# Ten of sixteen output-projection steps put inside the attention, and the value product one head at a time

## Chip, cores, metric

The kernel runs on one core of one Trainium2 chip. The metric is the device time of one execution in microseconds.

## What is computed

One inference step of a small hybrid decoder (two layers, width 1024) for a prompt of 512 tokens and 64 sample tokens (8 sequences of 8, each with 256 cached positions in pages). The change touches the first layer's mixer: eight heads of forgetting attention beside a gated recurrence, both halves multiplied by one output weight. Cut to what matters:

```python
s = einsum("bqhd,bkhd->bhqk", q, k) * scale
s = s + c_q - c_k                                    # running sums of log forget gates
prob = softmax(where(mask, s, NEG))
attn = einsum("bhqk,bkhd->bqhd", prob, v)
y_rg = h * gelu(gate)
merged = concatenate([attn, y_rg], axis=-1)          # 512 + 512 columns
x = x + einsum("bte,ed->btd", merged, w_out)
```

Products are in float32 accuracy: an operand is split into a high part and the rest, and high times high, high times low and low times high are summed.

## The kernel before

The text below names lines of the kernel before; in the kernel after, the same code stands further down. Tokens lie along the free dimension: `xT` holds 8 chunks of 128 model columns for 576 tokens, halved into 2 x 288. A program writes the order of instructions per engine; a scheduler shifts them by when it takes them to be ready, and each engine then works in that order.

The mixer's last stretch has three parts in program order.

1. *First half of the output projection* (`out_proj` with `k0 = 4`): weight rows that belong to the recurrence (`yh`, `yl`, the high and low parts of `y_rg`). For each of 8 output chunks `m`, `mm3` issues 24 matmuls of 128x288 (L132), and `add_x` adds the two halves to `xT` (VectorE, L658). Weights arrive as 1 MB (`raw`) and are split for two chunks at a time: a cast on ScalarE (L119), the rest on VectorE (L120), into a buffer `whl` of a pool with two buffers. Ahead of it, ScalarE and VectorE make the values' high and low parts (L461 to L463), and GpSimd builds the bias of the sample scores (L848 to L851).
2. *Attention*: 16 units, each one column `c` of two heads and one block `i` of 128 queries, `i` in the order 2, 3, 0, 1. In round n the code issues the scores of unit n (L787 the main product, L788 the gate sums through `kB`, L789 the mask), the softmax (VectorE L793, ScalarE L794, VectorE L795 and L796), then `p_trans` of unit n-1 (transposes L807, split into `ph` and `pl` by L809 and L810), then `p_out` of unit n-2: the value product (L821: for each key block `vh`x`ph`, `vl`x`ph`, `vh`x`pl`, both heads of the column against both heads' probabilities, 256 columns; half of the output is not used) and its split into `ah`, `al` (L829, L830). `kB` takes both buffers of the `whl` pool, four heads each. Between these pieces a list `side` spreads the sample group's attention: page loads by GpSimd (L743), their transposes (L873), products (all through L856), query copies on GpSimd (L762) and the transposes of its output (`sov`, L937).
3. *Second half of the output projection* (`k0 = 0`) over `ah`, `al`, again L132; chunk by chunk it hands on to the next norm.

Of the kernel before, what the change touches and what calls it, by code (L numbers as in the profile page):

```python
# [8 lines left out]
F32 = mybir.dt.float32  # L9
F32R = mybir.dt.float32r  # L10
# [8 lines left out]
P = 128  # L19
D = 1024  # L20
NP = 512
# [22 lines left out]
class Trunk:  # L44
# [343 lines left out]
    def mixer_ab(self):  # L388
# [3 lines left out]
        with tc.tile_pool(name="mix", bufs=1, reuse_waits="tile") as mp, ExitStack() as att:  # L392
# [8 lines left out]
            with tc.tile_pool(name="yy", bufs=1, reuse_waits="tile") as yp:  # L401
                with tc.tile_pool(name="rg", bufs=1, reuse_waits="tile") as rp:
# [7 lines left out]
                    for a in range(2):  # L410
                        for j, t in enumerate((self.xgh[a], self.xgl[a])):
# [57 lines left out]
                def prepare(m):  # L469
                    if m == 3:  # L470
                        q2s[2] = self.p_split(mp, *self.UNITS[2])
                    if m == 5:
# [256 lines left out]
    def k_rows(self, kT, ck, a):  # L729


        kB = self.wh.tile([P, 4, NP], F32R, name="kB", tag="whl")

        def step(h):
            self.nc.vector.tensor_copy(kB[0:64, h], kT[0:64, 4 * a + h, :])
            self.nc.scalar.copy(kB[64:68, h], ck[32 * h:32 * h + 4, a, :])

        return kB, [lambda h=h: step(h) for h in range(4)]
# [25 lines left out]

    UNITS = [(c, i) for c in range(4) for i in (2, 3, 0, 1)]


    def attention(self, mp, aq, q2s, zs, kT, cq, ck, vh, vl, qn, kn, vs, lf, ds, ah, al):
        nc, I = self.nc, self.I
        V, A, G, PE = nc.vector, nc.scalar, nc.gpsimd, nc.tensor  # L770
        with self.tc.tile_pool(name="at", bufs=2, reuse_waits="tile") as ap:
# [3 lines left out]
            kBs, ksteps = zip(*[self.k_rows(kT, ck, a) for a in range(2)])  # L775
            for f in ksteps[0]:
                f()
            obank = {}

            def p_scores(c, i, z):  # L780
# [3 lines left out]
                for e in range(2):  # L784
# [3 lines left out]
                    PE.matmul(s[:, 0:n], z[0:68, 1, e], kBs[h // 4][0:68, h % 4, 0:n], start=False, stop=False)  # L788
# [11 lines left out]
            def p_trans(c, i, es):  # L800
                n = (i + 1) * P
                ph = ap.tile([P, 4, 2, P], F32R, name="ph", tag="ph")
                pl = ap.tile([P, 4, 2, P], F32R, name="pl", tag="pl")
                for e in range(2):
                    pe = self.bank()
                    for k in range(i + 1):
                        PE.transpose(pe[:, k * P:(k + 1) * P], es[e][:, k * P:(k + 1) * P], self.ident)  # L807
                    pv = pe[:, 0:n].rearrange("p (k q) -> p k q", q=P)
                    A.copy(ph[:, 0:i + 1, e, :], pv)  # L809
                    V.tensor_tensor(pl[:, 0:i + 1, e, :], pv, ph[:, 0:i + 1, e, :].bitcast(F32), SUB)  # L810
                return ph, pl

            def p_out(c, i, ph, pl):
                if i % 2 == 0:
                    obank[0] = self.bank()
                o = obank[0]
                u = slice(i % 2 * 256, i % 2 * 256 + 256)
                cs = slice(c * P, (c + 1) * P)
                for k in range(i + 1):
                    for j, (v, p) in enumerate(((vh, ph), (vl, ph), (vh, pl))):  # L820
                        PE.matmul(o[:, u], v[:, k, cs], p[:, k].rearrange("p e q -> p (e q)"),  # L821
                                  start=(k == 0 and j == 0), stop=(k == i and j == 2))
                if i % 2 == 1:
                    t0 = (i - 1) * P
                    for e in range(2):
                        r = slice(e * 64, (e + 1) * 64)
                        src = o[r].rearrange("p (i e q) -> p i e q", i=2, e=2)[:, :, e, :]
                        dh, dl = [t[r, c, t0:t0 + 256].rearrange("p (i q) -> p i q", i=2) for t in (ah, al)]
                        A.copy(dh, src)  # L829
                        V.tensor_tensor(dl, src, dh.bitcast(F32), SUB)  # L830
# [12 lines left out]
            bn = one(full, "bn")  # L843
# [126 lines left out]
            for h in range(4):  # L970
                at(3 + h, ksteps[1][h])
            q1 = q2 = None
            for n in range(len(units) + 2):
# [14 lines left out]
                q1, q2 = nxt, t2  # L988

# [529 lines left out]
```

## Time and profile before

| | |
|---|---|
| median of 3 runs | 1306.14 us (1304.78 to 1307.19) |
| the profiled execution: time | 1310.66 us |
| the profiled execution: span from first to last instruction | 1308.9 us |
| mean granted TensorE clock | 0.995 |
| first half of the output projection | about 181.0 to 208.6 us |
| attention | about 208.6 to 296.3 us |

The profile is of one execution. A window row gives a stretch, its length, how long TensorE, its weight load, VectorE (DVE), ScalarE (ACT) and GpSimd (POOL) were busy in it with the number of instructions, then the granted TensorE clock, the DMA share and GB/s; a timeline row gives start, length and, in brackets, how long the engine sat idle just before and what released it. Lengths of matmuls overlap, so their rate is read from starts or from a count over a stretch.

### The profile page before, as it was taken

How to read it: one execution, taken by the hardware profiler on the slowest of the kernel's cores; microseconds unless marked ns; L12 is line 12 of the kernel's file. 1: busy time of each engine (PE TensorE's matmuls, PEld its weight loads, DVE VectorE, ACT ScalarE, POOL GpSimd, SP SyncE). 2: the span in 40 equal slices, each digit the busy share in tenths (PEclk: the TensorE clock that was granted, in tenths of full speed). 3: DMA queues.
4: the chain of work that ended last, by engine and by line, in shares of the span. 5: the costliest groups of instructions: out<-in, count | busy, mean ns of one | idle time of the engine just before them, and what ended most of it. 6: DMA issues, size and time to landing. Idle time of an engine off the chain costs nothing.

```text
span 1308.9 us, 23023 instructions
## 1 busy us (share of the span) xinstructions
PE 1288.2 (98%) x9462; PEld 1233.3 (94%) x9462; DVE 813.9 (62%) x1559; ACT 532.8 (41%) x877; POOL 167.4 (13%) x527
## 2 busy tenths in 40 slices
PE   8999999999999999999999999999999999999998
PEld 6987888779999999999999999899999999999998
DVE  6847847887767635765367657776743666346742
ACT  6656445674433313332133335444321343124421
POOL 2240053446100000000000002210000000000000
PEclk9999999999999999999999999899999999999999
DMA  6223232424233132312321212232223222223121
GB/s 175 85 67 101 78 130 81 122 60 130 71 100 105 38 97 97 99 65 68 110 83 36 66 50 82 84 131 66 68 67 129 65 82 70 79 97 99 34 92 49
DMA packets 105918, 111.64 MB, mean 85 GB/s; under 512 B 6722, under 2 KB 96970, under 8 KB 105805
## 3 DMA queue, kind: packets, MB, share of 16 engines
q1 hardware_dynamic: 101668, 101.68, 24.2%
q0 software_dynamic: 3072, 8.46, 2.3%
q8 instruction: 74, 1.21, 0.4%
q14 instruction: 32, 0.25, 0.1%
q10 hardware_dynamic: 1072, 0.04, 0.1%
HBM read 104.14 MB, written 6.25 MB: 84 GB/s over the span
## 4 chain that ended last, share of the span: by engine, by line
PE 90%; DVE 5%; ACT 3%; issue 1%; DMA 0%; ACTq 0%
PE mmb L132 77%; PE mmb L564 4%; PE mmb L856 2%; DVE whl L120 1%; PE mmb L821 1%; PE mmb L346 1%; PE mmb L807 1%; DVE xl L282 0%; ACT zh L1098 0%; ACT whl L119 0%; DVE xl L463 0%; PE mmb L494 0%; PE mmb L570 0%; DVE xT L1128 0%; ACT eb L794 0%
## 5 line engine op out<-in xcount | busy, mean ns | idle before, releaser
L132 PE MATMUL mmb<-xh,whl 128*128 128x288 f32 x3456 | 616.5, 298 | 3.3 <-DVE whl L120 1.7
L132 PEld LDWEIGHTS mmb<-xh,whl 128*128 128x128 f32 x3456 | 513.9, 190 | 7.0 <-DVE whl L120 2.2
L132 PE MATMUL mmb<-xl,whl 128*128 128x288 f32 x1728 | 372.6, 297 | 1.6 <-DVE xl L282 1.6
L119 ACT CAST whl<-wraw 128x1024 fp32r<-128x1024 f32 (+1 forms) x176 | 183.1, 1041 | 374.0 <-PE mmb L132 271.6
L132 PEld LDWEIGHTS mmb<-xl,whl 128*128 128x128 f32 x1728 | 280.1, 190 | 2.1 <-DVE xl L282 2.1
L132 PE MATMUL mmb<-hh,whl 128*128 128x288 f32 x1536 | 271.2, 297 | 0.1
L120 DVE TENSOR_TENSOR whl<-wraw,whl 128x1024 fp32r<-128x1024 f32 (+1 forms) x176 | 214.7, 1220 | 79.6 <-ACT whl L119 74.2
L132 PEld LDWEIGHTS mmb<-hh,whl 128*128 128x128 f32 x1536 | 226.2, 188 | 0.7 <-ACT hh L1237 0.6
L132 PE MATMUL mmb<-hl,whl 128*128 128x288 f32 x768 | 165.0, 296 | 0.0
L658 DVE TENSOR_TENSOR xT<-mmb,xT 128x288 f32<-128x288 f32 x128 | 52.6, 452 | 158.9 <-PE mmb L132 158.6
L1217 DVE TENSOR_TENSOR u<-mmb,rb 128x288 f32<-128x288 f32 x96 | 44.0, 458 | 135.4 <-PE mmb L132 127.4
L1222 POOL COPY ut<-u 128x18 f32<-128x18 f32 x96 | 23.1, 241 | 782.3 <-DVE u L1219 782.3
L132 PEld LDWEIGHTS mmb<-hl,whl 128*128 128x128 f32 x768 | 123.1, 188 | 0.0
L1237 ACT CAST hh<-hf 128x576 fp32r<-128x576 f32 x48 | 32.3, 674 | 139.0 <-DVE hf L1234 139.0
L1226 ACT ACTIVATE t<-u,par 128x592 f32<-128x592 f32 x96 | 84.6, 881 | 3.6 <-POOL u L1221 2.0
L1228 DVE SCALAR_TENSOR_TENSOR t<-u,par,t 128x592 f32<-128x592 f32 x96 | 80.1, 835 | 3.4
L1227 DVE SCALAR_TENSOR_TENSOR t<-u,par,t 128x592 f32<-128x592 f32 x96 | 79.6, 830 | 1.1 <-ACT t L1226 1.0
L1231 ACT ACTIVATE t<-t 128x592 f32<-128x592 f32 x48 | 33.6, 699 | 95.0 <-DVE t L1228 95.0
L1238 DVE TENSOR_TENSOR hl<-hf,hh 128x576 fp32r<-128x576 f32 x48 | 36.4, 759 | 34.8 <-ACT hh L1237 34.8
L564 PE MATMUL mmb<-whl,xh 128*128 128x512 f32 x192 | 53.7, 400 | 0.0
L564 PEld LDWEIGHTS mmb<-whl,xh 128*128 128x128 f32 x192 | 35.9, 191 | 8.2
L1218 DVE TENSOR_TENSOR u<-mmb,rb 128x224 f32<-128x224 f32 x96 | 36.6, 382 | 0.0
(383 smaller groups left out, 1311.4 us busy)
## 6 DMA issues: line engine op xcount, KB each, us to landing
wraw<-in_ffn_w_up SPq DMA_DIRECT2D x48, 1024.0 KB
wraw<-in_ffn_w_down SPq DMA_DIRECT2D x24, 1024.0 KB
wraw<-in_ab_w_in SPq DMA_DIRECT2D x9, 1024.0 KB
wraw<-in_ab_w_out SPq DMA_DIRECT2D x4, 1024.0 KB
xt<-in_x_prompt SPq DMA_DIRECT2D x4, 512.0 KB
out_y_p<-y SPq DMA_DIRECT2D x8, 256.0 KB
wraw<-in_ab_w_in SPq DMA_DIRECT2D x2, 512.0 KB
out_k_p<-X SPq DMA_DIRECT2D x1, 1024.0 KB
```

The lines of the kernel that those rows point to most:

```text
L119: keep(self.nc.scalar.copy(hi, v))
L120: keep(self.nc.vector.tensor_tensor(lo, v, hi.bitcast(F32), SUB))
L132: nc.tensor.matmul(ps[hf][:, 0:HT], w[:, k, :], x[:, hf * HT:(hf + 1) * HT], start=(n == 0 and j == 0), stop=(n == K - 1 and j == 2))
L564: PE.matmul(ps[i], x[:, i * P:(i + 1) * P], w[:, k2, :], start=(k == 0 and j == 0), stop=(k == 7 and j == 2))
L658: self.nc.vector.tensor_tensor(x, ps[hf][:, 0:HT], x, ADD)
L1217: V.tensor_tensor(u[:, 2:2 + HT], ps[0][:, 0:HT], self.rb[:, 0:HT], MUL)
L1218: V.tensor_tensor(u[:, 2 + HT:514], ps[1][:, 0:NP - HT], self.rb[:, HT:NP], MUL)
L1226: A.activation(t, u[:, 2:594], AF.Identity, scale=self.fw(l, 2, ch), bias=self.fb(l, ch))
L1227: V.scalar_tensor_tensor(t, u[:, 1:593], self.fw(l, 1, ch), t, MUL, ADD)
L1228: V.scalar_tensor_tensor(t, u[:, 0:592], self.fw(l, 0, ch), t, MUL, ADD)
L1231: A.activation(tg[:, 0:592], tg[:, 0:592], AF.Gelu_apprx_tanh)
L1238: V.tensor_tensor(hl, hf_, hh.bitcast(F32), SUB)
```

## The change

- The first half of the projection is made of 16 steps (`out_steps`): a chunk and a half of the tokens, 12 matmuls, one bank, one addition. Six run ahead of the attention. Ten are issued inside it, one each in rounds 4, 5, 6, 8, 10, 12, 14, 15, 16 and 17, right after the scores. The weight split is made per chunk (512 columns) into one buffer `fw`, double-buffered inside; `kB` has the other buffer of the pool, holds four heads, and is written over head by head.
- The value product goes one head at a time. A key block's weights are the high and low parts of one head side by side (`v2`, 2 x 64 columns), so `ph` and `pl` each pass once; two query blocks go together (256 columns, 128 for the last key block, whose first query block is masked). The two 64-row halves of the output are added afterwards: a copy on ScalarE and an addition on VectorE per head, then one split into `ah`, `al` for both. It runs before `p_trans` of the next unit, and for odd `i` only.
- The descriptor scratch of GpSimd's DMAs is set to 2048 bytes, and the sample bias `bn` moves to another pool.

```diff
@@ mixer_ab @@
-                vh, vl = [self.half(n, 1).rearrange("p c t -> p (c t)")[:, 0:2048].rearrange("p (i d) -> p i d", i=4)
-                          for n in ("xh", "xl")]
+                v2 = [t.rearrange("p c t -> p (c t)")[:, i * 1024:(i + 1) * 1024].rearrange("p (h s d) -> p h s d", h=H, s=2)
+                      for t in (self.half("xh", 1), self.half("xl", 1)) for i in range(2)]
...
-                    A.activation(vh[:, i, :], pv[i], AF.Identity, scale=sc)
+                    hd = lambda t: t.rearrange("p (h d) -> p h d", h=H)
+                    A.activation(v2[i][:, :, 0], hd(pv[i]), AF.Identity, scale=sc)
                     A.activation(vt[:, i, :], pv[i], AF.Identity, scale=sc)
-                    V.tensor_tensor(vl[:, i, :], vt[:, i, :], vh[:, i, :].bitcast(F32), SUB)
+                    V.tensor_tensor(v2[i][:, :, 1], hd(vt[:, i, :]), v2[i][:, :, 0].bitcast(F32), SUB)
...
-                self.out_proj(lambda k: (yh[:, k, :], yl[:, k, :]), 4, range(8), prepare)
-            self.attention(mp, aq, q2s, zs, kT, cq, ck, vh, vl, qn, kn, vs, lf, ds, ah, al)
-            att.close()
+                kB = self.wh.tile([P, 4, NP], F32R, name="kB", tag="whl")
+
+                fill = self.out_steps(lambda k: (yh[:, k, :], yl[:, k, :]), 4, range(8), prepare)
+                for _ in range(2 * self.AHEAD):
+                    fill.popleft()()
+                self.attention(mp, aq, q2s, zs, kT, cq, ck, v2, qn, kn, vs, lf, ds, ah, al, kB, fill)
+                att.close()
@@ new function @@
+    def out_steps(self, xs, k0, order, after):
+
+        w = self.I["ab_w_out"][0].rearrange("(k p) n -> p k n", p=P)
+        now = {}
+
+        fw = self.wh.tile([P, 2, 2, 512], F32R, name="fw", tag="whl")
+
+        def step(m, hf):
+            if hf == 0 and m % 4 == 0:
+                now["r"] = self.raw(w[:, k0:k0 + 4, m * P:m * P + 512], 4, 512)
+            hi, lo = [fw[:, m % 2, a].rearrange("p (k n) -> p k n", k=4) for a in range(2)]
+            if hf == 0:
+                v = now["r"][:, :, m % 4 * P:m % 4 * P + P]
+                self.nc.scalar.copy(hi, v)
+                self.nc.vector.tensor_tensor(lo, v, hi.bitcast(F32), SUB)
+            ps = self.bank()
+            for k in range(4):
+                xh, xl = xs(k)
+                for j, (a, x) in enumerate(((hi, xh), (hi, xl), (lo, xh))):
+                    self.nc.tensor.matmul(ps[:, 0:HT], a[:, k, :], x[:, hf * HT:(hf + 1) * HT],
+                                          start=(k == 0 and j == 0), stop=(k == 3 and j == 2))
+            x = self.xT[:, m, hf * HT:(hf + 1) * HT]
+            self.nc.vector.tensor_tensor(x, ps[:, 0:HT], x, ADD)
+            if hf:
+                after(m)
+
+        return deque([lambda m=m, hf=hf: step(m, hf) for m in order for hf in range(2)])
@@ k_rows, one head at a time @@
+    def k_rows(self, kB, kT, ck, h):
+
+        self.nc.vector.tensor_copy(kB[0:64, h % 4], kT[0:64, h, :])
+        self.nc.scalar.copy(kB[64:68, h % 4], ck[32 * (h % 4):32 * (h % 4) + 4, h // 4, :])
@@ attention @@
+    AHEAD = 3
+    FILL = (4, 5, 6, 8, 10, 12, 14, 15, 16, 17)
...
-                ph = ap.tile([P, 4, 2, P], F32R, name="ph", tag="ph")
-                pl = ap.tile([P, 4, 2, P], F32R, name="pl", tag="pl")
+                if i % 2 == 0:
+                    pair[c, i // 2] = [ap.tile([P, 4, 2, 2, P], F32R, name=nm, tag=nm, bufs=1) for nm in ("ph", "pl")]
+                ph, pl = pair[c, i // 2]
...
             def p_out(c, i, ph, pl):
+
                 if i % 2 == 0:
-                    obank[0] = self.bank()
-                o = obank[0]
-                u = slice(i % 2 * 256, i % 2 * 256 + 256)
-                cs = slice(c * P, (c + 1) * P)
-                for k in range(i + 1):
-                    for j, (v, p) in enumerate(((vh, ph), (vl, ph), (vh, pl))):
-                        PE.matmul(o[:, u], v[:, k, cs], p[:, k].rearrange("p e q -> p (e q)"),
-                                  start=(k == 0 and j == 0), stop=(k == i and j == 2))
...
+                    return
+                o = self.bank()
+                for e in range(2):
+                    for k in range(i + 1):
+                        w = v2[k][:, 2 * c + e].rearrange("p s d -> p (s d)")
+                        q0 = P if k == i else 0
+                        for j, p in enumerate((ph, pl)):
+                            PE.matmul(o[:, e * 256 + q0:e * 256 + 256], w,
+                                      p[:, k, e].rearrange("p i q -> p (i q)")[:, q0:256],
+                                      start=(k == 0 and j == 0), stop=(k == i and j == 1))
+                t = self.sm.tile([P, T], F32, name="fo", tag="dgs", bufs=1)[:, 0:256]
+                for e in range(2):
+                    r, x = [slice(a * 64, (a + 1) * 64) for a in (e, 1 - e)]
+                    u = slice(e * 256, e * 256 + 256)
+                    A.copy(t[r], o[x, u])
+                    V.tensor_tensor(t[r], o[r, u], t[r], ADD)
+                dh, dl = [x[:, c, (i - 1) * P:(i + 1) * P] for x in (ah, al)]
+                A.copy(dh, t)
+                V.tensor_tensor(dl, t, dh.bitcast(F32), SUB)
...
             for h in range(4):
-                at(3 + h, ksteps[1][h])
+                at(4 + 4 * (h // 2) + h % 2, lambda h=h: self.k_rows(kB, kT, ck, 4 + h))
...
                 step(k)
+                if n in self.FILL:
+                    fill.popleft()()
+                if q2:
+                    p_out(*q2)
                 t2 = (q1[0], q1[1], *p_trans(*q1)) if q1 else None
                 step(k)
-                if q2:
-                    p_out(*q2)
...
-    nc = bacc.Bacc("TRN2", target_bir_lowering=False, num_devices=1)
+    nc = bacc.Bacc("TRN2", target_bir_lowering=False, num_devices=1, dynamic_dma_scratch_size=2048)
```

How the order of instructions moves is shown at three places. In the kernel after, L683 is the addition of a step, L675 the `fw` split, L680 its matmuls, L855 the value product, L863 and L866 the addition and split of its output.

VectorE, ahead of the attention, before (`xl<-vt` is the values' low part, `xT` an addition, `whl` a weight split of two chunks):

```order
L722 COPY z<-cq 4x128 x4
L463 TENSOR_TENSOR xl<-vt,xh 128x512 x3
L658 TENSOR_TENSOR xT<-mmb,xT 128x288 x2
L463 TENSOR_TENSOR xl<-vt,xh 128x512
L725 CAST z<-mmb 64x256 x2
L120 TENSOR_TENSOR whl<-wraw,whl 128x1024
L658 TENSOR_TENSOR xT<-mmb,xT 128x288 x2
L710 TENSOR_TENSOR q_1991<-X,q_1991 128x2x64
L120 TENSOR_TENSOR whl<-wraw,whl 128x1024
```

and after:

```order
L756 COPY z<-cq 4x128 x4
L465 TENSOR_TENSOR xh<-vt,xh 128x8x64 x2
L465 TENSOR_TENSOR xl<-vt,xl 128x8x64
L683 TENSOR_TENSOR xT<-mmb,xT 128x288 x2
L465 TENSOR_TENSOR xl<-vt,xl 128x8x64
L759 CAST z<-mmb 64x256 x2
L744 TENSOR_TENSOR q_1905<-X,q_1905 128x2x64
L683 TENSOR_TENSOR xT<-mmb,xT 128x288 x2
L675 TENSOR_TENSOR fw<-wraw,fw 128x512
L744 TENSOR_TENSOR q_2032<-X,q_2032 128x2x64
L683 TENSOR_TENSOR xT<-mmb,xT 128x288
L675 TENSOR_TENSOR fw<-wraw,fw 128x512
```

The split that the third chunk needs (the first `fw` row here) still stands behind the values, the query copies and the additions of two chunks; it is half as wide.

VectorE, from the last unit's softmax to the end of the attention, before:

```order
L795 RECIPROCAL st<-st 128x1
L120 TENSOR_TENSOR whl<-wraw,whl 128x1024
L796 TENSOR_SCALAR eb<-eb,st 128x256
L795 RECIPROCAL st<-st 128x1
L810 TENSOR_TENSOR pl<-mmb,ph 128x128
L796 TENSOR_SCALAR eb<-eb,st 128x256
L830 TENSOR_TENSOR xl<-mmb,xh 64x256
L947 TENSOR_TENSOR xl<-mmb,xh 64x4x2x8
L810 TENSOR_TENSOR pl<-mmb,ph 128x2x128 x2
L830 TENSOR_TENSOR xl<-mmb,xh 64x256
```

and after:

```order
L822 TENSOR_REDUCE st<-mmb 128x1 x2
L120 TENSOR_TENSOR whl<-wraw,whl 128x1024
L824 RECIPROCAL st<-st 128x1 x2
L683 TENSOR_TENSOR xT<-mmb,xT 128x288
L825 TENSOR_SCALAR eb<-eb,st 128x256 x2
L863 TENSOR_TENSOR fo<-mmb,fo 64x256
...
L683 TENSOR_TENSOR xT<-mmb,xT 128x288
L120 TENSOR_TENSOR whl<-wraw,whl 128x1024
L863 TENSOR_TENSOR fo<-mmb,fo 64x256 x2
L866 TENSOR_TENSOR xl<-fo,xh 128x256
```

An addition of a step has come between the reciprocals and the scalings, and a second weight split stands ahead of the last three operations on `fo`.

TensorE, the tail of the attention, before (`sov` is the sample output, `eb` the probabilities of a prompt unit):

```order
L821 MATMUL mmb<-pl,xh 128x256
L807 MATMUL mmb<-ident,eb 128x128
L821 MATMUL mmb<-ph,xh 128x256
L821 MATMUL mmb<-ph,xl 128x256
L821 MATMUL mmb<-pl,xh 128x256
L937 MATMUL mmb<-ident,sov 128x128 x4
L807 MATMUL mmb<-ident,eb 128x128 x4
L821 MATMUL mmb<-ph,xh 128x256
L821 MATMUL mmb<-ph,xl 128x256
L821 MATMUL mmb<-pl,xh 128x256
```

and after:

```order
L855 MATMUL mmb<-pl,xl 128x128
L838 MATMUL mmb<-ident,eb 128x128 x2
L973 MATMUL mmb<-ident,sov 128x128 x4
L680 MATMUL mmb<-yh,fw 128x288
L680 MATMUL mmb<-yl,fw 128x288
...
L680 MATMUL mmb<-yh,fw 128x288
L838 MATMUL mmb<-ident,eb 128x128 x4
L680 MATMUL mmb<-yh,fw 128x288
L680 MATMUL mmb<-yl,fw 128x288
...
L855 MATMUL mmb<-pl,xh 128x128
L132 MATMUL mmb<-xh,whl 128x288 x2
```

Between the `sov` transposes and the last value product two steps of the projection (24 matmuls of L680) have come in; before, the wait for the probabilities lay there. The second half (L132) now begins only behind the last value product.

## Rows read from the trace of the kernel before

**Rows 1.** The page, busy us of the engines (share, instructions).

```profile
PE 1288.2 (98%) x9462; PEld 1233.3 (94%) x9462; DVE 813.9 (62%) x1559; ACT 532.8 (41%) x877; POOL 167.4 (13%) x527
```

**Rows 2.** Busy windows, projection's first half: stretch, length, us busy by engine.

```profile
181.00:188.00 7.00, 7.00 (x55) 6.87 (x52) 6.32 (x9) 5.37 (x11) 6.50 (x5) 1.00 0.43 154
188.00:190.00 2.00, 0.28 (x2) 0.18 (x2) 1.97 (x4) 1.77 (x3) 1.69 (x2) 1.00 0.49 121
190.00:208.60 18.60, 18.60 (x141) 18.60 (x142) 8.79 (x20) 5.08 (x9) 4.98 (x11) 1.00 0.47 163
```

**Rows 3.** Busy windows of the attention, cut at units 0, 4, 8, 12.

```profile
209.40:225.40 16.00, 15.71 (x138) 12.79 (x137) 14.18 (x46) 13.12 (x40) 5.69 (x12) 1.00 0.22 67
225.40:250.00 24.60, 24.06 (x233) 18.66 (x231) 22.30 (x69) 16.64 (x54) 11.12 (x18) 1.00 0.39 107
250.00:275.10 25.10, 24.27 (x261) 19.30 (x259) 20.24 (x62) 16.66 (x56) 7.01 (x8) 1.00 0.27 76
275.10:296.30 21.20, 18.77 (x181) 14.19 (x179) 18.73 (x57) 14.97 (x48) 13.12 (x55) 1.00 0.32 100
```

**Rows 4.** Timeline of TensorE at 190 us: start, us, instructions [wait, releaser].

```profile
189.82 0.81 PE L132 MATMUL mmb<-yh,whl 128*128 128x288 f32 x4 [1.72 <-DVE whl L120]
```

**Rows 5.** Timeline of VectorE, 180 to 190 us.

```profile
180.32 0.92 DVE L722 CAST z<-cq 4x128 fp32r<-4x128 f32 x4 [2.15 <-ACT vs L451]
...
186.89 0.84 DVE L463 TENSOR_TENSOR xl<-vt,xh 128x512 fp32r<-128x512 f32 x1
187.76 0.75 DVE L725 CAST z<-mmb 64x256 fp32r<-64x256 f32 x2
188.54 1.23 DVE L120 TENSOR_TENSOR whl<-wraw,whl 128x1024 fp32r<-128x1024 f32 x1
189.68 0.82 DVE L658 TENSOR_TENSOR xT<-mmb,xT 128x288 f32<-128x288 f32 x2
```

**Rows 6.** Timeline of ScalarE, query casts and kB copies.

```profile
188.21 0.70 ACT L726 CAST z<-mmb 64x256 fp32r<-64x256 f32 x2 [1.84 <-DVE z L725]
...
208.79 2.50 ACT L736 CAST kB<-ck 4x512 fp32r<-4x512 f32 x4 [3.87 <-PE mmb L132]
```

**Rows 7.** VectorE's groups by line and shape: count, busy us, mean ns.

```profile
L658 DVE TENSOR_TENSOR xT<-mmb,xT 128x288 f32<-128x288 f32 x128 | 52.6, 452 | 158.9 <-PE mmb L132 158.6
...
L830 DVE TENSOR_TENSOR xl<-mmb,xh 64x256 fp32r<-64x256 f32 x16 | 6.7, 418 | 1.2 <-ACT xh L829 1.0
...
L463 DVE TENSOR_TENSOR xl<-vt,xh 128x512 fp32r<-128x512 f32 x4 | 5.2, 1337 | 0.6 <-ACT vt L462 0.6
...
L120 DVE TENSOR_TENSOR whl<-wraw,whl 128x512 fp32r<-128x512 f32 x4 | 2.8, 690 | 0.0
```

**Rows 8.** The chain of waits in the attention: start, us, what.

```profile
272.63 1.41 PE mmb L821 x12
```

**Rows 9.** Timeline of TensorE, score matmuls of 128 columns.

```profile
263.51 0.27 PE L788 MATMUL mmb<-kB,z 68*128 68x128 f32 x1
263.63 0.23 PE L789 MATMUL mmb<-maskb,identb 128*128 128x128 bf16 x1
```

**Rows 10.** Timeline of TensorE in the tail of the attention.

```profile
288.67 0.23 PE L789 MATMUL mmb<-maskb,identb 128*128 128x128 bf16 x1
...
292.53 0.41 PE L807 MATMUL mmb<-ident,eb 128*128 128x128 f32 x2 [1.45 <-DVE st L795]
...
293.85 0.29 PE L132 MATMUL mmb<-xh,whl 128*128 128x288 f32 x1
...
295.87 0.29 PE L132 MATMUL mmb<-xh,whl 128*128 128x288 f32 x1
...
296.32 0.67 PE L132 MATMUL mmb<-xh,whl 128*128 128x288 f32 x3 [0.16 <-ACT xh L946]
```

**Rows 11.** Timeline of GpSimd, sample bias and query copies.

```profile
182.38 1.59 POOL L851 TENSOR_TENSOR bd<-cbs,ds 128x512 f32<-128x512 f32 x1
...
195.37 1.65 POOL L762 COPY qz<-qn 64x16 f32<-64x16 f32 x7 [4.56 <-DMA cache_v<-in_cache_v,pidx]
```

More of the change, by code (lines that the diff above doesn't have):

```diff
@@ L727, in p_prep @@
         return z
[L729 to L738, printed above, removed]
+    def k_rows(self, kB, kT, ck, h):
+        self.nc.vector.tensor_copy(kB[0:64, h % 4], kT[0:64, h, :])
+        self.nc.scalar.copy(kB[64:68, h % 4], ck[32 * (h % 4):32 * (h % 4) + 4, h // 4, :])
     def page(self, pool, src, j, bufs):
@@ L763, in s_queries, with attention @@
                                            qn[r, c, pr * 16:(pr + 1) * 16].rearrange("p (b t) -> p b t", b=2))
+    AHEAD = 3
+    FILL = (4, 5, 6, 8, 10, 12, 14, 15, 16, 17)
     UNITS = [(c, i) for c in range(4) for i in (2, 3, 0, 1)]
-    def attention(self, mp, aq, q2s, zs, kT, cq, ck, vh, vl, qn, kn, vs, lf, ds, ah, al):
+    def attention(self, mp, aq, q2s, zs, kT, cq, ck, v2, qn, kn, vs, lf, ds, ah, al, kB, fill):
         nc, I = self.nc, self.I
@@ L774, in attention @@
             units = self.UNITS
[L775 to L778, printed above, removed]
+            for h in range(4):
+                self.k_rows(kB, kT, ck, h)
+            pair = {}
             def p_scores(c, i, z):
@@ L787, in p_scores @@
                     PE.matmul(s[:, 0:n], z[:, 0, e], kT[:, h, 0:n], start=True, stop=False)
-                    PE.matmul(s[:, 0:n], z[0:68, 1, e], kBs[h // 4][0:68, h % 4, 0:n], start=False, stop=False)
+                    PE.matmul(s[:, 0:n], z[0:68, 1, e], kB[0:68, h % 4, 0:n], start=False, stop=False)
                     PE.matmul(s[:, qs], self.identb, self.maskb, start=False, stop=True)
@@ L808, in p_trans @@
                     pv = pe[:, 0:n].rearrange("p (k q) -> p k q", q=P)
-                    A.copy(ph[:, 0:i + 1, e, :], pv)
-                    V.tensor_tensor(pl[:, 0:i + 1, e, :], pv, ph[:, 0:i + 1, e, :].bitcast(F32), SUB)
+                    hi, lo = [t[:, 0:i + 1, e, i % 2, :] for t in (ph, pl)]
+                    A.copy(hi, pv)
+                    V.tensor_tensor(lo, pv, hi.bitcast(F32), SUB)
                 return ph, pl
@@ L814, in p_out @@
                 if i % 2 == 0:
-                    obank[0] = self.bank()
-                o = obank[0]
-                u = slice(i % 2 * 256, i % 2 * 256 + 256)
-                cs = slice(c * P, (c + 1) * P)
-                for k in range(i + 1):
-                    for j, (v, p) in enumerate(((vh, ph), (vl, ph), (vh, pl))):
-                        PE.matmul(o[:, u], v[:, k, cs], p[:, k].rearrange("p e q -> p (e q)"),
-                                  start=(k == 0 and j == 0), stop=(k == i and j == 2))
[L823 to L830, printed above, removed]
+                    return
[17 more added lines that the diff above has]
+                V.tensor_tensor(dl, t, dh.bitcast(F32), SUB)
             one = lambda shape, nm, dt=F32: aq.tile(shape, dt, name=nm, tag=nm, bufs=1)
@@ L842, in attention @@
             bd = one([P, 2, NB, H, NT], "bd")
-            bn = one(full, "bn")
+            bn = self.sm.tile([P, NB, H, NT], F32, name="bn", tag="sq", bufs=2)[0:NS]
             def s_setup():
@@ L983, in attention @@
                 step(k)
+                if n in self.FILL:
+                    fill.popleft()()
+                if q2:
+                    p_out(*q2)
                 t2 = (q1[0], q1[1], *p_trans(*q1)) if q1 else None
                 step(k)
-                if q2:
-                    p_out(*q2)
                 q1, q2 = nxt, t2
+            while fill:
+                fill.popleft()()
     def pool_setup(self, pb):
```

4 lines of the change are left out of this document (2 added, 2 removed).

## Prediction

> **What bounds the kernel now.** The first part of the page says that TensorE is busy for 98% of the span [rows 1], so a change can only gain where TensorE waits or where it is given less to do. Everything that is moved lies between 181.0 and 296.3 us, and I read that region by its windows first and by the timelines after. In the projection's first half TensorE is full but for two microseconds: between 188 and 190 us it works 0.28 us while VectorE works 1.97 [rows 2]. In the attention I cut the windows at the first score matmul of units 0, 4, 8 and 12. TensorE is idle for 0.29, 0.54, 0.83 and 2.43 us of the four stretches, 4.1 us together, and VectorE is busy for 89, 91, 81 and 88% of them [rows 3]. So the attention is a stretch in which two engines are nearly full at once. That is the point to keep: filling TensorE's holes costs VectorE work, and VectorE has little room.
>
> Then the timelines. From 190 us to the end of the first half, 141 matmuls take 18.60 us [rows 2], 0.132 each; a step (one chunk of 128 output columns, one half of the tokens, 12 matmuls) is 1.6 us. The stall at 188 us ends at 189.82 with VectorE's weight split L120 [rows 4], which starts at 188.54 because VectorE had the low parts of the values (L463) and the query copies (L725) ahead of it [rows 5].
>
> **Stretch 1, before the attention: -15.2 us.** Ten of sixteen steps leave it. The other six keep their pace, but the stall stays. Four steps end at 181.0 + 4 x 1.60 = 187.4. The fifth needs the third weight split, `fw`. On ScalarE its cast stands behind the query casts that end at 188.9 [rows 6]; on VectorE it stands behind L463, L725, a query split and the two additions of the second chunk, which as in [rows 5] end near 189.6. The split of 512 columns is 0.69 us [rows 7], so TensorE goes on at about 190.25, against 189.82 before. Two more steps end at 193.4. The old end is 208.6, 16 steps and the stall after 181.0 [rows 2]. The four copies of kB that now come earlier fall into the 2.15 us in which VectorE waited for `vs` [rows 5]; I cost them at nothing. Without that cover each would be about 0.4 us, as the half-width L830 is [rows 7].
>
> **Stretch 2, units 0 to 3: -0.9 us.** There is no fill here. The value product of units 0 and 1 gets shorter. Twelve old products take 1.41 us [rows 8], 0.118 each. Per column of heads the old code has 30 of 256 columns; the new one has 16 of 256 and 8 of 128. No row has just this product at 128 columns, so I bound it: half of 0.118 from below (0.059), 0.12 from above, the step from one 128-column matmul to the next in the scores [rows 9]. I take 0.12, since the row has the same width and type. A pair of units (2,3) then goes from 21 x 0.118 = 2.48 to 1.90, a pair (0,1) from 1.06 to 0.95: 0.58 and 0.11 less, 2.8 us over the attention (4.7 at the other bound). The first pair (2,3) falls into this stretch: -0.58. Before, four kB copies of ScalarE also stand ahead of the first exponential, from 208.79 for 2.50 us [rows 6]; they are no longer there. Since TensorE is idle for only 0.29 us of this stretch, I count half of that and 0.2 for the copies; the bound is the whole 1.9 us from 209.4 to 211.3.
>
> **Stretch 3, units 4 to 7: +3.85 us.** Three fills are 4.8 us of TensorE. Two value products give back 0.69, and I let half of the 0.54 us of waits be filled. VectorE gets three additions (0.45 us each [rows 7]), two `fw` splits and two extra half additions of L863 (0.42 each by L830 [rows 7]); one 1.23-us split of the second projection half, which stood here, moves to the end. That is 22.3 + 2.3 = 24.6 us in 28.4, 87% against 91% before, so VectorE doesn't become the bound.
>
> **Stretch 4, units 8 to 11: +2.1 us.** Two fills, 3.2, less 0.69 for the products and half of 0.83.
>
> **Stretch 5a, units 12 to 14 up to the last scores at 288.8: +2.8 us.** Two fills, 3.2, less 0.11 and half of the 0.55 us of waits that lie here.
>
> **Stretch 5b, the tail: +2.3 us.** Before, 288.8 to 296.3 is 7.5 us, in which nine matmuls (1.2 us) of the second half were already done [rows 10]. TensorE's order after is: fill 1.6, 16 products 1.9, two transposes 0.2, four `sov` transposes 0.4, fill 1.6, four transposes 0.45, fill 1.6, eight products 0.95. Together 8.7 us, and 8.7 + 1.2 - 7.5 = 2.3. Three fills (4.8) thus cost 2.3: here is the 1.45-us wait for L795 [rows 10], a reciprocal that stands behind a split L120 in VectorE's queue, and the first fill covers it. VectorE has some 7.1 us of work ahead of the last products: the split 1.2, two fill additions 0.9, three operations on `fo` 1.2, some 3.8 for softmax, probability splits and small copies (estimated from the 0.42 of a half-width operation [rows 7]). TensorE comes to these products after 7.75 us. What comes late next is the last L866: a split of the second half (1.23) and three new operations on `fo` stand ahead of it, near 10.4 us. The matmuls that read it come from 11.1 us on, so I add nothing; without that cover it costs up to 0.5.
>
> **Sum.** -15.2 - 0.9 + 3.85 + 2.1 + 2.8 + 2.3 = -5.05 us. The profiled execution took 1310.7 us and would take 1305.6; the median of the runs is 4.5 us lower, and the same difference taken off it gives 1306.1 - 5.05 = **1301.0 us**. The smaller descriptor scratch I cost at nothing: the page loads keep their order on GpSimd and never have many in flight. If GpSimd had to wait for one page per pair of units, the page that qz waited for (4.56 us [rows 11]) shows the size.
>
> **A rule against the change.** While GpSimd ran L851 and its neighbours, L463 took 1.34 us on average, where a split of as many columns takes 0.69 [rows 7, 11]. The Trainium skill ("SBUF — State Buffer", section "SBUF: two separate sides") says that a VectorE operation with two SBUF inputs and a GpSimd operation that reads SBUF shut each other out of a shared port. The rows agree. Four `fw` splits now run in the attention, where GpSimd is busy for 37 of 87 us [rows 3]. At L463's price they cost VectorE 4 x 0.65 = 2.6 us more. My sum has 0.69; all of 2.6 on the path would give 1303.6.
>
> **The rivals.** *All waits are filled.* TensorE's work is the only bound: -15.2 + 16.0 - 2.8 - 4.1 = -6.1, with the kB copies' 1.9 us -8.0, 1298.1 us; down to 1296 if 128 columns cost half. For it speaks that the fills stand right behind the scores, in the time of the exponentials. Against it: VectorE's share [rows 3].
> *The waits stay.* VectorE, fed with ten additions, four splits and eight extra additions, keeps TensorE as idle as before: -15.2 + 16.0 - 2.8 = -2.0, 1304.1 us.
> *The port.* The splits slowed by GpSimd, as above: 1303.6 us.
> *Slower.* The additions of the fills hold up VectorE's queue. Four of the ten stand directly ahead of a reciprocal or a scaling that the next transposes need, the others ahead of a reduction or a probability split; each waits for the end of its fill, 1.6 us after the scores. A reduction and an exponential take about as long, so the addition should find its fill done. If TensorE's own delays make it wait, and each of the ten holds TensorE for half a fill, it is +8, 1309 us. It decides from 0.5 us per fill on. Against it: TensorE hardly waits where VectorE is 91% busy [rows 3].
>
> **How the numbers follow.** My forecast (1299 to 1303) has a chance of 0.50, all waits filled 0.16, the waits stay 0.17, the port 0.07, slower 0.10. A measurement of this kernel tells about 0.2%, 2.6 us, from no change. Faster by more than that, below 1303.5: the forecast, the full filling and half of the port's and a little of the waits' case, 0.72. Slower, above 1308.8: with the larger mishaps of the queue, 0.09. Within: 0.19. The range 1296 to 1306 leaves out the slower case and little below the full filling; the forecast's own is 1299 to 1303.
>
> **What would show it.** The first score matmul should stand near 194.4 us (one microsecond of sample scores is ahead of it), and the dense second half should begin at 291.3 us rather than 296.3. The idle time of TensorE from there on should be near 2 us; if it is 4 or more, the waits stayed, and the waits' view names VectorE's L683 or L795 for the queue, L675 at over 1 us for the port. The products L855 should be 12 + 4 in 1.9 us. I am wrong if the restart near 190 us moves by over 1 us, if page transposes wait for GpSimd in units 0 to 3 (before, GpSimd's query copies end at 197 us [rows 11], and the next pages can be issued only behind them), or if the last L866 is what the second half waits for.

## The result, and the profile after

The changed kernel takes 1299.9 us (median of five runs, 1298.1 to 1300.8) against 1306.1 us: ratio 0.9949, 95% interval 0.9938 to 0.9960, so 6.2 us faster. Run once more beside the experiments it came to 0.9956 (0.9939 to 0.9973). One execution of a variant below (a step in front of the page) took 4330.1 us and is left out of its ratio.

The first line of the profile's page, against [rows 1]: TensorE has less work, and it fills more of the span.

```profile
PE 1281.7 (99%) x9438; PEld 1229.2 (95%) x9438; DVE 816.6 (63%) x1571; ACT 537.0 (41%) x889; POOL 165.6 (13%) x527
```

Busy windows of the same region after. The first three rows answer to [rows 2] (two chunks of steps, the stall, the last two steps), the others to [rows 3], with the tail cut once more at the last scores.

```profile
180.48:186.95 6.47, 6.47 (x51) 6.39 (x49) 5.57 (x6) 5.36 (x11) 5.95 (x5) 1.00 0.48 170
186.95:189.00 2.05, 0.17 (x3) 0.02 (x1) 1.99 (x7) 1.27 (x4) 1.74 (x2) 1.00 0.26 64
189.00:196.26 7.26, 7.26 (x32) 7.26 (x33) 2.01 (x5) 3.23 (x6) 3.66 (x11) 0.53 0.26 76
196.26:211.35 15.09, 14.77 (x132) 11.90 (x131) 14.31 (x44) 12.46 (x37) 6.13 (x13) 1.00 0.51 171
211.35:238.05 26.70, 26.70 (x263) 22.29 (x262) 25.28 (x78) 19.30 (x61) 11.80 (x18) 1.00 0.33 94
238.05:264.21 26.16, 26.00 (x278) 21.22 (x277) 22.68 (x69) 18.06 (x58) 7.05 (x8) 1.00 0.27 77
264.21:277.37 13.16, 13.16 (x153) 10.57 (x152) 12.64 (x38) 10.13 (x33) 7.23 (x32) 1.00 0.55 162
277.37:286.75 9.38, 9.38 (x76) 9.09 (x75) 8.85 (x26) 7.27 (x20) 8.71 (x31) 1.00 0.14 42
```

Two things are to be seen. From unit 4 on TensorE is idle for 0.16 us in 75, although VectorE is busy for 92% of that time. And the third row has a granted clock of 0.53: behind the stall TensorE ran at its 1.2 GHz level. All that TensorE waits for between 190 and 300 us, but for waits under 0.1 us, is this (the waits' view: engine and line, what it waited for, total, times, longest):

```profile
PE mmb L838 <- DVE eb L825: 0.3, 1, 0.3
PE mmb L892 <- ACT kt L911: 0.2, 1, 0.2
```

The stall itself, in TensorE's timeline after, which answers to [rows 4]:

```profile
186.81 0.29 PE L680 MATMUL mmb<-yh,fw 128*128 128x288 f32 x1
188.98 0.51 PE L680 MATMUL mmb<-yh,fw 128*128 128x288 f32 x1 [1.88 <-ACT fw L674]
189.28 0.45 PE L680 MATMUL mmb<-yl,fw 128*128 128x288 f32 x1
...
195.31 0.44 PE L680 MATMUL mmb<-yl,fw 128*128 128x288 f32 x1
195.55 0.61 PE L680 MATMUL mmb<-yh,fw 128*128 128x288 f32 x2
196.00 0.30 PE L680 MATMUL mmb<-yl,fw 128*128 128x288 f32 x1
196.13 0.30 PE L680 MATMUL mmb<-yh,fw 128*128 128x288 f32 x1
196.26 0.34 PE L816 MATMUL mmb<-kT,z 128*128 128x384 f32 x1
```

Its starts are 0.24 us apart where at 196 us, and before the stall, they are 0.13 apart. The bracket names ScalarE's cast L674, since the first matmuls of a step read only the high part.

To compare kernels I cut each trace at the same instructions: first step, first score matmul, units 4, 8 and 12, last scores, and the first matmul of the next norm (L252). Lengths in us. "Again" is the second profiled execution of the changed kernel; the others are the experiments below.

| | before | changed | again | no steps inside | old product | steps early |
|---|---|---|---|---|---|---|
| first step to first score | 28.4 | 15.8 | 14.3 | 28.6 | 12.6 | 12.7 |
| units 0 to 3 | 16.0 | 15.1 | 15.5 | 15.2 | 16.7 | 15.8 |
| units 4 to 7 | 24.6 | 26.7 | 26.5 | 24.9 | 28.1 | 28.6 |
| units 8 to 11 | 25.1 | 26.2 | 26.0 | 23.8 | 26.7 | 29.1 |
| unit 12 to last scores | 13.3 | 13.2 | 13.2 | 12.9 | 15.2 | 14.4 |
| last scores to next norm | 45.1 | 48.0 | 48.2 | 46.7 | 47.2 | 45.4 |
| sum | 152.5 | 144.9 | 143.6 | 151.9 | 146.4 | 145.9 |

The region gives 7.6 and 8.9 us, the runs 6.2 and 5.8 (5.8 by the ratio; the two medians of the second comparison, 1303.0 and 1310.4, lie 7.4 apart). The rest of the kernel is the same program, and single executions differ there: from the next norm to the end it took 975.5, 972.8 and 975.5 us in the first three columns, with 6.8, 3.4 and 6.8 us at the lower clock between 817 and 841 us. A difference of a microsecond between two columns is not evidence.

### The profile page after: what moved, and what is told of

Same layout as the page of the kernel before. It is cut to its first block, busy times and chain, and to the rows that moved or that the text cites. A ratio compares the mean times of both kernels' runs of the same rounds, so it can differ in the third digit from the quotient of the medians.

```text
span 1298.2 us, 22971 instructions
## 1 busy us (share of the span) xinstructions
PE 1281.7 (99%) x9438; PEld 1229.2 (95%) x9438; DVE 816.6 (63%) x1571; ACT 537.0 (41%) x889; POOL 165.6 (13%) x527
## 4 chain that ended last, share of the span: by engine, by line
PE 78%; DVE 4%; ACT 2%; issue 1%; ACTq 0%
PE mmb L132 72%; PE mmb L892 1%; PE mmb L680 1%; PE mmb L855 1%; PE mmb L838 1%; DVE xl L282 0%; ACT zh L1138 0%; DVE whl L120 0%; PE mmb L909 0%; PE mmb L1221 0%; ACT whl L119 0%; DVE xT L1168 0%; DVE zl L1139 0%; PE mmb L816 0%; PE mmb L817 0%
## 5 line engine op out<-in xcount | busy, mean ns | idle before, releaser
L132 PE MATMUL mmb<-xh,whl 128*128 128x288 f32 x3456 | 614.3, 298 | 1.9 <-DVE whl L120 1.4
L132 PEld LDWEIGHTS mmb<-xh,whl 128*128 128x128 f32 x3456 | 511.7, 189 | 5.4 <-DVE whl L120 1.9
L132 PE MATMUL mmb<-xl,whl 128*128 128x288 f32 x1728 | 371.3, 296 | 0.5 <-DVE xl L282 0.5
L119 ACT CAST whl<-wraw 128x1024 fp32r<-128x1024 f32 (+1 forms) x172 | 178.9, 1041 | 366.6 <-PE mmb L132 265.8
L132 PEld LDWEIGHTS mmb<-xl,whl 128*128 128x128 f32 x1728 | 279.3, 189 | 0.7 <-DVE xl L282 0.7
L132 PE MATMUL mmb<-hh,whl 128*128 128x288 f32 x1536 | 271.4, 297 | 0.1
L120 DVE TENSOR_TENSOR whl<-wraw,whl 128x1024 fp32r<-128x1024 f32 (+1 forms) x172 | 209.8, 1220 | 77.7 <-ACT whl L119 77.5
L132 PEld LDWEIGHTS mmb<-hh,whl 128*128 128x128 f32 x1536 | 226.2, 189 | 0.7 <-ACT hh L1277 0.6
L132 PE MATMUL mmb<-hl,whl 128*128 128x288 f32 x768 | 165.1, 296 | 0.0
L692 DVE TENSOR_TENSOR xT<-mmb,xT 128x288 f32<-128x288 f32 x112 | 46.1, 453 | 150.1 <-PE mmb L132 149.8
L132 PEld LDWEIGHTS mmb<-hl,whl 128*128 128x128 f32 x768 | 123.2, 189 | 0.0
```

The source lines that it names most:

```text
L119: keep(self.nc.scalar.copy(hi, v))
L120: keep(self.nc.vector.tensor_tensor(lo, v, hi.bitcast(F32), SUB))
L132: nc.tensor.matmul(ps[hf][:, 0:HT], w[:, k, :], x[:, hf * HT:(hf + 1) * HT], start=(n == 0 and j == 0), stop=(n == K - 1 and j == 2))
```

## The experiments

The theory: TensorE's work in the ten steps fills its waits in the attention, and once it has none left, it alone sets the pace there; a shorter value product then counts in full. The rivals: the gain is the product's alone; or the steps only trade places. "The changed kernel again" below is the changed kernel in its second set of runs. Ratios are to the kernel before, run on the same chip (its median there 1310.6 us for the first four, 1310.4 for the rest).

**No steps inside.** `AHEAD = 8`, `FILL = ()`; the new product, key rows and all else stay.

> The changed kernel with all sixteen steps of the first half in front of the attention again; the value product by heads, the key rows and everything else stay. Theory (the time comes from the steps' 1.6 us each filling waits of TensorE in the attention): the ten steps cost their full time in front, first score near 209, the waits of 2 to 3 us per unit pair come back, and only the product's gain of about 2.8 us stays: 1303 to 1305 us, a ratio to before near 0.998. Rival (the gain is the product's and the earlier key rows', the moved steps only trade places): near the changed kernel's 1300 us, ratio 0.995.

Measured: 1.0010 (0.9994 to 1.0025). The steps are needed for the gain; with the product alone no gain shows in the runs, where the theory had 2.8 us. Its windows from unit 4 on:

```profile
225.86:250.75 24.89, 23.15 (x227) 17.72 (x226) 22.67 (x72) 18.54 (x60) 11.88 (x18) 1.00 0.36 102
250.75:274.53 23.78, 23.00 (x255) 18.15 (x253) 22.23 (x68) 17.00 (x56) 7.71 (x8) 1.00 0.30 84
274.53:287.39 12.86, 11.25 (x127) 7.76 (x126) 11.77 (x35) 9.98 (x32) 7.12 (x32) 0.92 0.33 84
287.39:294.58 7.19, 6.30 (x33) 5.64 (x33) 5.48 (x18) 4.82 (x17) 6.47 (x22) 0.67 0.37 119
```

TensorE is idle for 5.0 us here, where [rows 3] has 3.8: part of what the product saves has turned into waits for VectorE and ScalarE. Another part is the clock. From the first step to the last scores the table has 105.3 us against 107.4, 2.1 less and near the theory; then the clock fell at 285.4 us for 6.8 us, and the end took 1.6 us more. The runs show it too: the mean granted clock of these 12 runs is 0.992, of the kernel before beside them 0.995, and among the 12 the one at 0.995 took 1305.0 us and the one at 0.989 took 1315.3. The 25 runs of the kernel before that stand beside the later experiments go from 1306.3 us at 0.997 to 1313.8 at 0.990, about 1 us for each 0.001; by that, an estimate, 3 to 4 us of the time here belong to the clock. So what the product is worth alone at an equal clock isn't shown; some 2 us fit.

**The old product, with the steps inside.**

```diff
-    w = v2[k][:, 2 * c + e].rearrange("p s d -> p (s d)")
-    PE.matmul(o[...], w, p[:, k, e]..., ...)
+    for j, (v, p) in enumerate(((vh, ph), (vl, ph), (vh, pl))):
+        PE.matmul(o[:, u], v[:, k, cs], p[:, k].rearrange("p e q -> p (e q)"), ...)
```

> The changed kernel with the ten steps inside the attention as they are, but the value product of before: 256 columns, both heads at a time, three matmuls per block instead of two stacked ones per head. Theory (TensorE now sets the pace of the attention, the product's matmuls are 0.118 us per 256 columns and about 0.12 or less per 128): slower than the changed kernel by 2.8 us where a 128-column matmul costs 0.12, up to 6 us where it costs the 0.06 to 0.09 that pairs of them showed: 1302.7 to 1306 us. Rival (the product lies in waits that VectorE and ScalarE leave, whose own work in it is no smaller now): no difference from 1299.9.

Measured: 0.9970 (0.9959 to 0.9981), 1.8 us behind the changed kernel run again, with intervals that overlap; since its mean clock also lies further under that of the kernel before beside it (0.9933 to 0.9954, against 0.9940 to 0.9950), about 1 us of the 1.8 may be the clock (an estimate, by the same 1 us for each 0.001). The region says it more sharply: 146.4 against 143.6 and 144.9, although the clock fell in the region of the changed kernel and not here. From unit 4 to the last scores it is 70.0 against 65.7 and 66.0 us, of which about 1.1 us is order (with the old product, unit 12's nine matmuls stand ahead of the last scores). In units 4 to 11, at full clock in all of them, the shorter product saves 2.0 to 2.3 us with the steps inside and 1.0 us without them. The old matmuls themselves show why: 78 of them take 9.53 us here from start to next start, 0.122 each. In the kernel before, 30 in units 4 to 7 took 5.35 (0.178 each) and 30 in units 8 to 11 took 4.56 (0.152). They weren't slower; short waits stood between them. Three of them before, the third 0.32 us behind the second with no idle time shown, and three here:

```profile
228.42 0.28 PE L821 MATMUL mmb<-ph,xl 128*128 128x256 f32 x1
228.54 0.28 PE L821 MATMUL mmb<-pl,xh 128*128 128x256 f32 x1
228.86 0.38 PE L821 MATMUL mmb<-ph,xh 128*128 128x256 f32 x1
```

```profile
215.15 0.28 PE L848 MATMUL mmb<-ph,xh 128*128 128x256 f32 x1
215.26 0.28 PE L848 MATMUL mmb<-ph,xl 128*128 128x256 f32 x1
215.38 0.28 PE L848 MATMUL mmb<-pl,xh 128*128 128x256 f32 x1
```

**Two more steps inside.** `AHEAD = 2`, `FILL = (2, 3, 4, 5, 6, 8, 10, 12, 14, 15, 16, 17)`.

> The changed kernel with two more steps moved: twelve inside the attention (two of them in units 2 and 3), four in front, so that the third weight split, for which TensorE waited 1.9 us at 187 and after which its granted clock was at the 1.2 GHz level for 6.8 us, no longer stands in front of the first score. Theory (TensorE bound in the attention; the stall and the half clock in front cost 2 plus 3.3 us): the two steps take 3.2 us in the attention as they did in front, less what waits are left there (about 0.5 us), and the stall and the slow clock go: 1295 to 1298 us. Rival (the split is late wherever it stands, or the wait moves to the first scores, whose queries are split by the same engines): 1299 to 1301, with a pause of 1 us or more between 187 and 200.

Measured: 0.9966 (0.9953 to 0.9979), no better than the changed kernel. By the ratio that is 1301.7 us against the 1306.1 of the result, outside the theory's 1295 to 1298 and just outside the rival's 1299 to 1301. The stall at 187 is gone and the first score comes 7.3 us behind the first step. But units 0 to 3 take 26.2 us instead of 15.1. Two steps are 3.2 of the difference; the longest of the new waits, behind which the clock fell for 3.4 us, is this:

```profile
202.59 0.63 PE L909 MATMUL mmb<-ident,cache_k 128*128 128x128 f32 x4 [3.89 <-DMA cache_k<-in_cache_k,pidx]
```

It is the fourth key page of the samples, and GpSimd's timeline in the same run shows why it is late:

```profile
188.30 1.28 POOL L771 DMA_INDIRECT cache_v<-in_cache_v,pidx  x1 [0.16 <-issue]
189.88 0.96 POOL L771 DMA_INDIRECT cache_v<-in_cache_v,pidx  x1 [0.30 <-issue]
190.85 0.20 POOL L790 COPY qz<-qn 64x16 f32<-64x16 f32 x1
193.77 1.92 POOL L790 COPY qz<-qn 64x16 f32<-64x16 f32 x7 [2.71 <-DMA cache_v<-in_cache_v,pidx]
196.29 0.98 POOL L771 DMA_INDIRECT cache_v<-in_cache_v,pidx  x1 [0.59 <-POOL qz L790]
197.57 0.96 POOL L771 DMA_INDIRECT cache_v<-in_cache_v,pidx  x1 [0.30 <-issue]
198.83 1.05 POOL L771 DMA_INDIRECT cache_k<-in_cache_k,pidx  x1 [0.30 <-issue]
```

The page is asked for behind four value pages and eight query copies, which themselves stand behind the sample bias and wait 2.7 us. In all six kernels that waited for it, the transposes began 21.8 to 23.0 us behind the first matmul of the gate sums (L732), whether the first score stood 8.7 or 15.7 us behind that matmul. It acts as a floor: an attention that begins sooner than the changed kernel's waits for this page until GpSimd's chain is shorter. The rival had a pause too, but earlier and for another cause.

**The queries' casts later.** They are put behind the split of the third chunk.

```diff
-    zs = {n: self.p_prep(aq, q2s[n], cq, *self.UNITS[n]) for n in range(2)}
...
-    for _ in range(2 * self.AHEAD):
+    for n in range(2 * self.AHEAD):
+        if n == 5:
+            zs = {u: self.p_prep(aq, q2s[u], cq, *self.UNITS[u]) for u in range(2)}
         fill.popleft()()
```

> The changed kernel with the casts of the first two units' queries put behind the split of the third weight chunk on ScalarE and VectorE instead of ahead of it; nothing else changes. Theory (the 1.9 us wait at 187 is for ScalarE, behind those casts, and the fall of the clock to the 1.2 GHz level belongs to that wait): no pause at 187, the clock stays at the 2.4 GHz level and the first score comes up to 5 us earlier, near 191 to 193: 1295 to 1298 us; if the first scores then wait 1 to 2 us for the queries, 1297 to 1299. Rival (the clock falls there for another reason, and the wait moves on to the first scores in full): 1299 to 1301.

Measured: 0.9924 (0.9905 to 0.9942), against 0.9956 (0.9939 to 0.9973) for the changed kernel again; the intervals touch, so a gain isn't shown. The region, 144.6 us with 0.4 us of query transposes that have come into it, lies between the two executions of the changed kernel (143.6 and 144.9). The two waits of TensorE:

```profile
191.63 0.53 PE L681 MATMUL mmb<-yh,fw 128*128 128x288 f32 x2 [1.25 <-DVE fw L676]
204.63 0.63 PE L910 MATMUL mmb<-ident,cache_k 128*128 128x128 f32 x4 [1.81 <-DMA cache_k<-in_cache_k,pidx]
```

The stall shrank from 1.88 to 1.25 us and the clock stayed up there, but the page took back what was won, and the clock fell behind that wait, at 205.7 us. The theory was right that the cast was late, but the next wait, for the split on VectorE, took 1.25 us of the 1.88; the gain that it forecast isn't shown.

**The changed kernel again.**

> The changed kernel itself, once more, on the chip of these runs, so that the variants are compared with it there. If the fall of the clock to the 1.2 GHz level behind the 1.9 us wait for the third weight split belongs to the change, it comes again at the same place and the first score follows the first step by 15.8 us, as before; if it is a matter of the single execution (two of the variants had the same wait without it), the first score comes after 12.6 us, and the transposes of the fourth key page are then waited for, 1 us or more. Ratio to before 0.994 to 0.996 either way.

Measured: 0.9956 (0.9939 to 0.9973). After the same stall of 1.88 us the clock fell again, for 3.4 us instead of 6.8, and the first score came 14.3 us behind the first step, between the two expected values. The page was already waited for:

```profile
187.75 0.40 PE L680 MATMUL mmb<-yh,fw 128*128 128x288 f32 x1 [1.88 <-ACT fw L674]
...
200.74 0.63 PE L909 MATMUL mmb<-ident,cache_k 128*128 128x128 f32 x4 [0.37 <-DMA cache_k<-in_cache_k,pidx]
```

**A step in front of the page.** With the casts later, and `FILL = (1, 4, 5, 6, 8, 10, 12, 14, 15, 16)`: unit 17's step is put into unit 1.

> The changed kernel with the queries' casts behind the third weight split, and one of the three steps of the end (unit 17's) put into unit 1. Theory (an early first score is no gain by itself, since the fourth key page lands near 204 whenever the scores begin, and TensorE waited 1.8 us for it in the variant with the later casts; a step put there costs nothing): the wait for the page falls under 0.5 us, unit 4 starts as late as without the step, and the end loses 1.6 us of work less what the step covered there, 0 to 1.6: 0 to 1.6 us faster than the variant with the later casts. Rival (the page's load is asked for later when TensorE is later, since its buffer must come free first, so that the wait moves along): 1.6 us later at unit 4 and the same total as that variant.

Measured: 0.9952 (0.9932 to 0.9972), no gain. The front did what the theory said: the wait for the page fell from 1.81 to 0.73 us, and although a step more lies ahead of it, unit 4 came 28.8 us behind the first step instead of 30.8. (Some 1.7 us of that, half of 3.4 and so an estimate, is the fall of the clock at 205.7, which did not come this time.) The tail gave it back, since the step taken out of it had covered a wait for the last probabilities:

```profile
283.51 0.39 PE L856 MATMUL mmb<-ph,xh 128*128 128x256 f32 x1 [2.10 <-ACT ph L842]
```

Behind it the clock fell for 3.4 us, and the end from the last scores took 49.9 us instead of 48.4.

**All ten steps in units 4 to 13.** `FILL = (4, 5, 6, 7, 8, 9, 10, 11, 12, 13)`.

> The changed kernel with the ten steps in ten successive units, 4 to 13, so that none stands behind the samples' work or after the last scores. Theory (in units 4 to 13 TensorE has no wait left, so a step there costs its full 1.6 us; after unit 13 the waits of the kernel without steps inside, some 3 us, come back): units 4 to 12 take 4.8 us more (three more steps), the end from the last scores 2 to 3 us less instead of 4.8: 2 to 3 us slower than the changed kernel. Rival (waits are spread evenly, any unit can take a step): no difference.

Measured: 0.9961 (0.9948 to 0.9975) and 1304.8 against 1303.0 us: the sign of the theory, within the intervals. The table shows the mechanism. Units 4 to 11 take 4.8 to 5.1 us more than in the changed kernel, for three more steps at 1.6, and the end 2.6 to 2.8 us less. Its last two windows show what then stands open:

```profile
269.29:283.65 14.36, 13.56 (x152) 10.56 (x152) 13.60 (x36) 10.31 (x31) 8.04 (x32) 1.00 0.27 75
283.65:289.37 5.72, 4.25 (x33) 3.49 (x33) 5.61 (x18) 4.96 (x17) 5.05 (x16) 1.00 0.09 24
```

TensorE is idle for 2.3 us here, and for none in the same two stretches of the changed kernel. Where a step stands does matter in the traces: in units 4 to 11 a third and fourth one costs its full price, at the end it costs part of it.

**The scratch alone.** The kernel before, with `dynamic_dma_scratch_size=2048`.

> The kernel before with the one edit that its descriptor scratch is 2048 bytes, as in the changed kernel. The prediction costs this edit at nothing: ratio 1.000 within 0.001, the GpSimd loads of the pages as far apart as before (0.95 to 1.3 us each). Rival (the smaller ring makes GpSimd wait until a load has landed before it can issue the next): the pages' loads 2 to 3 us apart and the kernel 2 us or more slower.

Measured: 1.0000 (0.9987 to 1.0012). It costs nothing that can be measured.

## Why the prediction was nearly right, step by step

The forecast of 1301.0 us, its range and its sign held, and the source of the gain is shown: without the steps inside no gain is measured, and without the new product units 4 to 11 take 2.0 to 2.3 us longer. But the sum came out near by errors of opposite sign, and the likeliest case was not the one that happened in the attention. Without the fall of the clock behind the stall, which the sum did not have, the region would be some 10.5 to 10.8 us shorter (an estimate: 8.9 + 1.6 and 7.6 + 3.2, from the first point below), twice the 5.05 of the sum. That the time came so near is in part luck.

- **Stretch 1: too much.** The first score was to come 15.0 us sooner; it came 12.6 and 14.2 us sooner, counted from the first step. I placed the end of the stall at VectorE's split; TensorE needs the cast alone for its first matmuls and went on 0.8 us earlier than I had it (8.5 us behind the first step, not 9.3). What I did not have is the fall of the clock behind the stall. Two experiments with the same stall and no fall have the first score after 12.6 and 12.7 us, 15.8 us sooner than before, so the fall cost 3.2 and 1.6 us in the two executions.
- **Stretch 2: right.** 0.9 predicted, 0.9 and 0.5 measured; in the second execution 0.37 is the page.
- **Stretches 3 and 4: too dear.** 3.85 and 2.1 predicted, 2.1 and 1.1 measured (1.9 and 0.9 again). "Half of the waits are filled" failed: all are. And the waits were longer than the idle time in [rows 3] that I halved. A busy matmul row reaches past the start of the next (0.28 us long, 0.12 apart), so a window counts a short wait as busy time. The starts show it: 60 old product matmuls took 9.9 us in these stretches of the kernel before, where 60 x 0.118 is 7.1. My unit price from the chain of waits [rows 8] was the price without waits.
- **Stretch 5a: a slip.** 2.8 predicted, 0.1 *less* measured. Before, 18 old matmuls stand here, after only 8 new ones: 2.1 against 0.95 us. I credited 0.11, while the tail's list already paid for the 16 that moved there, so 1.06 us was counted twice. The rest is filled waits, again: with each matmul at its mean step in the changed kernel, this stretch of the kernel before comes to 11.5 us of its 13.3, which leaves 1.8 us of waits (an estimate) where I had counted 0.55.
- **Stretch 5b: about right.** 2.3 predicted; up to the next norm 2.9 and 3.1 measured. The chain of waits of the changed kernel shows the order and the lengths that I had listed (start, us, what):

```profile
277.92 1.65 PE mmb L680 x12
279.58 1.80 PE mmb L855 x16
281.38 0.24 PE mmb L838 x2
281.62 0.44 PE mmb L973 x4
282.06 1.59 PE mmb L680 x12
283.65 0.44 PE mmb L838 x4
284.09 1.61 PE mmb L680 x12
```

- **The product: right.** 1.80 to 2.01 us for 16 of them were measured, 1.90 taken; that its value depends on who sets the pace was not in the sum.
- **The edits at nothing.** The scratch costs nothing that can be measured. VectorE's four kB copies ran from 176.5 to 178.7 us, and 1.7 us of its wait ahead of the values' split is left. The last L866 did not hold TensorE: it worked through 277.4 to 286.8 us without a gap and went on with L132.
- **The port: it did not come for the splits.** All eight took the same time (duration min/median/max in ns):

```profile
L675 DVE TENSOR_TENSOR fw<-wraw,fw x8: 680/684/694, 167.9 to 272.0; 128x512 fp32r<-128x512 f32 x8
L465 DVE TENSOR_TENSOR xl<-vt,xl x2: 836/1310/1784, 183.9 to 186.4; 128x512 fp32r<-128x512 f32 x2
```

The values' split again took up to 1.78 us, beside GpSimd's bias operations L885 and L887, which add two tensors. The four `fw` splits in the attention fell beside short query copies, page loads (twice) and memsets. It was GpSimd's copies that gave way:

```profile
188.98 0.68 DVE L675 TENSOR_TENSOR fw<-wraw,fw 128x512 fp32r<-128x512 f32 x1
189.38 0.33 POOL L790 COPY qz<-qn 64x16 f32<-64x16 f32 x1
```

This copy ended 0.05 us behind the split, and so did every one of the 17 query copies that began during an `fw` split in the eight traces with such splits (0.05 to 0.06 us behind it, up to 0.74 us long, where the median copy takes 0.19). That agrees with the Trainium skill ("SBUF — State Buffer", section "SBUF: two separate sides"), by which a VectorE operation with two SBUF inputs and a GpSimd operation that reads SBUF lock each other out. The share of GpSimd's busy time, by which I had priced it, is no measure of the cost: one must see which of its operations stands beside the split, and which of the two began first.
- **Of the rivals** *all waits are filled* described the attention; its 8.0 us gain is nearer to the region's 7.6 and 8.9 than my 5.05 (the runs' 6.2 is nearer to mine), and the fall of the clock hid part of it. *The waits stay* and *slower* are out: additions waited for their step four times, 4.2 us in all, and TensorE never for an addition. Of what would have made me wrong, the page transposes are there in small (0.37 us in one of two executions) and waited 0.52 to 3.89 us in the five variants whose first score comes sooner.

The fall of the clock behind the stall came in both executions of the changed kernel and in none of the three variants with the same stall. Why is open.

## What to carry to other kernels

Moving work into the waits of a nearly full engine paid although a second engine was 90% busy: from unit 4 to the last scores the first then had no wait longer than 0.16 us. Measure the waits from starts of instructions, since windows hide those shorter than the modelled length of a matmul. Two edits can be worth more together than apart: the shorter product saved 1.0 us of units 4 to 11 while its engine had waits, and 2.0 to 2.3 once they were filled. Read the granted clock of the runs beside their times: a variant with more waits can also run at a lower clock. And before bringing a stretch forward, look up the earliest time of everything that it consumes: here the fourth page, behind GpSimd's queue, is the next floor.

## What the runs showed of the hardware that I had not expected

Between 180 and 300 us the granted clock fell from the 2.4 to the 1.2 GHz level within 1.1 us behind single waits of TensorE: 1.88 us (changed kernel, both executions), 3.89, 1.81 and 2.10 us (two more steps inside, casts later, a step in front of the page). It stayed down for 3.4 us, once for 6.8, and the stretch in which it was down cost 1.6 and 3.2 us at the first place. In that stretch it did not fall behind 1.88 us in the three kernels with no steps inside, the old product and steps early, nor behind 1.72 and 1.45 us in the kernel before [rows 4, 10], nor behind any single wait of 1.25 us or less except near 285 us with no steps inside, where several short ones lay close together. A stall of 1.9 us thus cost 5.1 in one execution (1.9 + 3.2), and the same stall elsewhere cost itself alone.

The length of a single wait does not decide it, though. In the kernel before the clock fell 0.1 us behind a wait of 1.19 us, at 131.2 us; of the ten traces, all with a wait of 1.17 to 1.19 us at this place, one other shows the fall. And in all ten it fell between 167.6 and 171.7 us, for 3.4 us, although TensorE had not waited for more than 0.02 us in the 35 us before. There it came 0.0 to 1.4 us behind the last of 20 short matmuls (128x8, 0.11 us apart).
